# The start addresses of the SBUF tiles that TensorE reads, moved to multiples of 512 bytes

## The chip, the cores and the metric

One core of one Trainium2 chip runs the whole program. The metric is the device time of one execution in microseconds (us). Three runs of the kernel before took 2045.38, 2045.49 and 2047.89 us, with a median of 2045.49 us.

## The reference

A two-layer encoder trunk on 512 positions and 1024 channels, all in float32. One layer, cut to what matters here:

```python
hn = rmsnorm(x, norm_mix_g[l])
proj = hn @ w_in[l]                              # columns split among four mixers and four gates
ya, yb, yc, yd = mixer_a(...), mixer_b(...), mixer_c(...), mixer_d(...)
gates = sigmoid(gl.reshape(b, s, N_BRANCH, D_MODEL) + gate_bias[l])
merged = sum(gates[:, :, i] * (y_i @ w_proj_i[l]))
x = x + merged @ w_out[l]
hn = rmsnorm(x, norm_mlp_g[l])
x = x + square(relu(hn @ w_mlp1[l])) @ w_mlp2[l]  # 1024 -> 4096 -> 1024
```

Mixer A is dense attention, B a bidirectional linear recurrence, C windowed attention with a sink, D dilated windowed attention. A last RMSNorm ends the trunk.

## The kernel before

Activations lie in SBUF with channels on the 128 partitions and the 512 positions along the free dimension. A product of 1024 by 128 weights with the 512 positions is a chunk. Every weight matrix comes from HBM in chunks of 128 x 1024 numbers (`wload`, L102); ScalarE rounds a chunk to fp32r (`whi`, L118) and VectorE takes the remainder (`wlo`, L127). Activations are split the same way: `xh` and `xl` are the normalised input of the layer or of its MLP, `mh` and `ml` the merged mixers, the two `h` tiles of a quarter (`h0`, `h1`) the hidden MLP quarter, `y` with its two halves the output of a mixer. For each 128 contraction rows `mm3` then issues three matmuls, at full width of 512 columns:

```python
mm(ps, sh, mh, start=(k == 0), stop=False)    # L177  whi, high half of the activations
mm(ps, sh, ml, start=False, stop=False)       # L178  whi, low half
mm(ps, sl, mh, start=False, stop=(k == n - 1))  # L179  wlo, high half
```

The first operand after `ps` is the stationary one (128 columns of 4 bytes, 512 bytes of a partition, loaded by an LDWEIGHTS that the trace shows as PEld). The second is the moving one (512 columns, 2048 bytes of a partition). `several` (L193 to L195) issues the same three for two chunks in turns. An MLP chunk or an output chunk has 8 contraction steps, so 24 matmuls; a stage of 8 such chunks has 192.

The order of the work is fixed by the program. A layer has phase 1 (30 chunks with `xh` and `xl` moving, with rotary, convolution and recurrence beside them), the attention stages A, C and D, whose steps are merged with the gate chunks GL (`xh`, `xl` moving) and the branch projections PR (`y` moving) by `merge`, then the output stage OUT (`mh`, `ml` moving), then the MLP: the first half M1 (`xh`, `xl` moving) and the second half M2 (`h` moving) by quarters in the order M1(0) M1(1) M2(0) M1(2) M2(1) M1(3) M2(2) M2(3). In layer 1 the last two chunks of M2(3) run at half width (L1235 to L1237). Attention reads `Q`, `P`, `VV`, `VD`, `Qd` as stationary and `K`, `PT0`, `PT1`, `ptd`, `Kd` as moving tiles; its transposes (L835, L976) move the identity, a part of the constants `cs`, against a block of `P`.

Where a tile begins is set by the order and the sizes of the pools and tiles. The constants begin at byte 16512 of the partition. The tiles of pool `cp` before the weight pools are `cs`, `ve`, `ones`, `acc`, `rb`, `d_hb`, `d_lgb`, `d_sp`, `d_nsp` and `d_nsink`, the last one 64 bytes. They end at byte 27200, which is 53 x 512 + 64. Behind them lie the pools of `raw`, `whi` and `wlo`, `xh` and `xl`, the small tiles (`sm`), and the pools of the stages. Every chunk tile is a multiple of 512 bytes, so whatever offset the first has, the rest of that run of pools has too.

Of the kernel before, what the change touches and what calls it, by code (L numbers as in the profile page):

```python
# [11 lines left out]
F32 = mybir.dt.float32  # L12
F32R = mybir.dt.float32r
# [7 lines left out]
DM, S, DEPTH, HD = 1024, 512, 2, 64  # L21
EPS = 1e-6
NEG = -1e30
KD = DM // 128
# [51 lines left out]
class Body:  # L76
# [138 lines left out]
        return self.mm3(ps, self.wst(hl), self.xmv, KD, step)  # L215


    def smt(self, n, tag):
        return self.sm.tile([128, n], F32, tag=tag, name=tag)

    def rsqrt(self, v, n, tag):

# [54 lines left out]
    def setup(self):  # L277
        nc = self.nc
        cp = self.cp
        self.cs = cp.tile([128, NC_], F32, name="cs")  # L280
        self.ve = cp.tile([128, DEPTH * NV + 8], F32, name="ve")
        self.ones = cp.tile([128, 128], F32, name="ones")
        nc.sync.dma_start(out=self.ve, in_=self.vec)
        nc.vector.memset(self.ones, 1.0)
        nc.scalar.copy(self.ones[0:1, 0:1], self.ones[0:1, 0:1])
        self.ident = self.cs[:, C_ID:C_ID + 128]
        nl = DEPTH
        self.xh = self.xgp.tile([128, KD, S], F32R, name="xh")
        self.xl = self.xgp.tile([128, KD, S], F32R, name="xl")
        self.acc = cp.tile([128, S], F32, name="acc")  # L290
        self.rb = cp.tile([128, S], F32, name="rb")
        self.d_hb = cp.tile([128, nl, 32], F32, name="d_hb")
        self.d_lgb = cp.tile([128, nl, 16], F32, name="d_lgb")
        self.d_sp = cp.tile([128, nl, 8], F32, name="d_sp")
        self.d_nsp = cp.tile([128, nl, 8], F32, name="d_nsp")
        self.d_nsink = cp.tile([128, nl, 8], F32, name="d_nsink")

    def derive(self):
        nc = self.nc
        nv = nc.vector  # L300
        vv = self.ve[:, 0:DEPTH * NV].rearrange("p (l n) -> p l n", l=DEPTH)
        ts = nv.tensor_scalar
        ts(out=self.d_hb, in0=vv[:, :, V_GB:V_GB + 32], scalar1=0.5, scalar2=None, op0=ALU.mult)
        ts(out=self.d_lgb, in0=vv[:, :, V_LGB:V_LGB + 16], scalar1=0.5, scalar2=None, op0=ALU.mult)
        ts(out=self.d_nsink, in0=vv[:, :, V_SINK:V_SINK + 8], scalar1=-1.0, scalar2=None, op0=ALU.mult)

        n = DEPTH * 8
        sh = lambda t: t.rearrange("p (l n) -> p l n", l=DEPTH)
        lam = self.smt(n, "spl")
        ts(out=sh(lam), in0=vv[:, :, V_LAM:V_LAM + 8], scalar1=1.0, scalar2=None, op0=ALU.mult)  # L310
        mx, u, d, s, s2, p = (self.smt(n, "sp" + c) for c in "mudsqp")
        nv.scalar_tensor_tensor(out=mx, in0=lam, scalar=-1.0, in1=lam, op0=ALU.mult, op1=ALU.min)
        nc.scalar.activation(out=u, in_=mx, func=AF.Exp)
        ts(out=d, in0=u, scalar1=2.0, scalar2=None, op0=ALU.add)
        nv.reciprocal(out=d, in_=d)
        nv.tensor_tensor(out=s, in0=u, in1=d, op=ALU.mult)
        nv.tensor_tensor(out=s2, in0=s, in1=s, op=ALU.mult)
        ts(out=p, in0=s2, scalar1=1.0 / 17.0, scalar2=None, op0=ALU.mult)
        for k in (15, 13, 11, 9, 7, 5, 3):
            nv.scalar_tensor_tensor(out=p, in0=p, scalar=1.0 / k, in1=s2, op0=ALU.add, op1=ALU.mult)  # L320
        nv.scalar_tensor_tensor(out=p, in0=p, scalar=1.0, in1=s, op0=ALU.add, op1=ALU.mult)
        ts(out=mx, in0=lam, scalar1=-1.0, scalar2=0.0, op0=ALU.mult, op1=ALU.max)
        nv.scalar_tensor_tensor(out=p, in0=p, scalar=2.0, in1=mx, op0=ALU.mult, op1=ALU.add)
        ts(out=self.d_sp, in0=sh(p), scalar1=4.0, scalar2=None, op0=ALU.mult)
        ts(out=self.d_nsp, in0=sh(p), scalar1=-4.0, scalar2=None, op0=ALU.mult)

    def v(self, l, i):
        return self.ve[:, l * NV + i:l * NV + i + 1]
# [68 lines left out]
    def phase1(self, l):  # L397
        nc, p1 = self.nc, self.p1
# [3 lines left out]
        self.nrs8 = self.mixp.tile([128, 4], F32, tag="nrs8", name="nrs8")  # L402
        self.rs8p = self.mixp.tile([128, 4], F32, tag="rs8p", name="rs8p")
        self.rqs = self.mixp.tile([128, 4, 8], F32, tag="rqs", name="rqs")
        self.VV = self.mixp.tile([128, 4, 4, 128], F32R, tag="VV", name="VV")
        self.yB = self.y0p.tile([128, 2, 4, S], F32R, tag="y", name="yB")
        self.qsA = self.drp.tile([8, 128, S], F32, tag="qsA", name="qsA")
# [53 lines left out]
            self.derive()  # L461

        rd = self.drp.tile([S], F32, tag="rd", name="rd")
        self.roff = self.mixp.tile([128, 4], F32, tag="roff", name="roff")
        nc.sync.dma_start(out=rd.rearrange("(o n) -> o n", o=1), in_=row)
        nc.sync.dma_start(out=self.roff, in_=rd.rearrange("(p r) -> p r", r=4))
        self.conv_b(l, 0, X["bx", 0])
# [75 lines left out]
    def conv_b(self, l, f, ps):  # L543
        p1, nv, ns = self.p1, self.nc.vector, self.nc.scalar
        v = lambda i: self.v(l, i)
        bx = p1.tile([128, S + 4], F32, tag="bx", name="bx", bufs=4)
        nv.memset(bx[:, 0:2], 0.0)
        nv.memset(bx[:, S + 2:S + 4], 0.0)
        nv.tensor_tensor(out=bx[:, 2:S + 2], in0=ps, in1=self.rb, op=ALU.mult)
        xc = p1.tile([128, S], F32, tag="xc", name="xc", bufs=4)  # L550
        if f == 0:
            self.xcs, self.xch, self.bdone = {}, {}, set()
        self.xcs[f] = xc

        def tap(j):
            if j == 0:
                ns.activation(out=xc, in_=bx[:, 0:S], func=AF.Identity, scale=v(V_CW + f), bias=v(V_CB + f))
            else:
                nv.scalar_tensor_tensor(
                    out=xc, in0=bx[:, j:j + S], scalar=v(V_CW + 4 * j + f), in1=xc, op0=ALU.mult, op1=ALU.add  # L560
                )

        self.bq.append(lambda: tap(0))
        self.bq.append(lambda: (tap(1), tap(2)))
        self.bq.append(lambda: tap(3))
        if f < 2:
            self.bq.append(lambda: self.split_b(f))
# [321 lines left out]
    def attn_d(self, l, y):  # L889
        nc, ap = self.nc, self.ap  # L890
        nv, ns = nc.vector, nc.scalar
        QK, OG, PO = {}, {}, {}
        ML = [ap.tile([128, 4, 2, 4], F32, tag=f"ML{g}", name=f"ML{g}", bufs=1) for g in range(3)]
        mld = self.drp.tile([3, S, 8], F32, tag="mld", name="mld")
        wd = self.drp.tile([12, S], F32, tag="wd", name="wd")
        steps = []
# [11 lines left out]
        def step(g, h, u, first, last):  # L908
# [22 lines left out]
            def exps():  # L931
                ps = st["s"]
                P = st["P"] = ap.tile([128, S], F32, tag="P", name="P", bufs=4)
                if g == 0:
                    for w in range(2):
# [7 lines left out]
                        )  # L943
                        nm = ML[0][:, c, 0, h:h + 1]
                        nv.tensor_scalar(
# [3 lines left out]
                            out=Pw, in_=Pw, func=AF.Exp, scale=self.rs8[:, c:c + 1], bias=nm,  # L949
                            accum_out=ML[0][:, c, 1, h:h + 1],  # L950
                        )
                else:
# [5 lines left out]
                    nv.tensor_reduce(out=m, in_=P3, axis=AX.X, op=ALU.max, negate=True)  # L958
                    nv.tensor_tensor(out=ML[g][:, :, 0, h], in0=m, in1=self.rs8p, op=ALU.mult)
                    for r in range(4):  # L960
                        ns.activation(
                            out=P3[:, r], in_=P3[:, r], func=AF.Exp, scale=self.rs8p[:, r:r + 1],
                            bias=ML[g][:, r, 0, h:h + 1], accum_out=ML[g][:, r, 1, h:h + 1],
                        )
# [156 lines left out]
    def layer(self, l):  # L1121
# [27 lines left out]
            self.merge(self.attn_d(l, yD), self.fill(l, 2, yC), *MG[2])  # L1149
            self.merge(self.attn_d_end(yD), (next(fill) for _ in range(FN)), E1 + E2 + 1 + 2 * E3, FN)  # L1150
        mhp = pool(es_r, f"mh{l}", side="right")
        self.mh = mhp.tile([128, KD, S], F32R, name="mh")
        self.ml = mhp.tile([128, KD, S], F32R, name="ml")
        self.run(fill)
        es_mix.close()

# [21 lines left out]
        hp = pool(es_m, f"h{l}")  # L1178
        tp = pool(es_m, f"t{l}", 2)
        r2 = xp.tile([128, S], F32, name="r2")  # L1180
        H = {}

        def m1(q):
            H[q] = [hp.tile([128, KD, S], F32R, tag=f"h{z}", name=f"h{z}", bufs=2) for z in range(2)]
            early = self.several([("M1", 0, c) for c in range(2)], self.xmv, (6,)) if q == 0 else []
            for c in range(KD):
                if early:
                    ps = early.pop(0)
                else:
                    hl = self.take("M1", q, c)  # L1190
                    ps = self.wide()
                    self.run(self.proj8(hl, ps))
                if q == 0 and c == 3:
                    pv = self.misc()
                    nc.tensor.matmul(pv, self.ones, self.acc)
                    nv.tensor_scalar(out=r2, in0=pv, scalar1=1.0 / DM, scalar2=EPS, op0=ALU.mult, op1=ALU.add)
                    nv.reciprocal(out=r2, in_=r2)
                r = tp.tile([128, S], F32, tag="r", name="r")
                ns.activation(out=r, in_=ps, func=AF.Relu)
                nv.scalar_tensor_tensor(out=r, in0=ps, scalar=0.0, in1=r, op0=ALU.max, op1=ALU.mult)  # L1200
                self.split(r, H[q][0][:, c], H[q][1][:, c])
# [19 lines left out]
        def last(h):  # L1221
# [70 lines left out]
            store(1, 0, KD)  # L1292

        m1(0)
        m1(1)
        m2(0)
# [181 lines left out]
```

## Time and profile before

| | before |
|---|---|
| median of 3 runs | 2045.49 us |
| the profiled execution | 2045.1 us |
| its span, first to last instruction | 2043.3 us |
| mean granted clock of TensorE | 0.996 |
| TensorE matmul busy (PE) | 2023.1 us, 99% |
| weight loads busy (PEld) | 1664.0 us, 81% |
| VectorE (DVE), ScalarE (ACT) busy | 1270.7 us, 62%; 975.0 us, 48% |

The profiled execution's span leaves 1.8 us of its time outside. A matmul in these rows has a modelled end and overlaps the next one, so the duration of one is longer than the distance from its start to the next start. The rate of TensorE is read from the length of a stretch and the number of matmuls that begin in it.

### The profile page before, as it was taken

The page shows a single profiled execution, that of the slowest core. Times are in us where ns is not written, and L with a number is a line of the kernel's source. Part 1 is how long each engine was busy: PE and PEld are TensorE (multiplying, and loading weights), DVE is VectorE, ACT ScalarE, POOL GpSimd, SP SyncE. Part 2 cuts the span into 40 slices and gives each one's busy share as a digit, 9 for nine tenths or more (in the row PEclk, how much of TensorE's full clock was granted, in tenths as well). Part 3 has the DMA queues.
Part 4 walks back from the last instruction along what each step waited for, and adds up shares of the span by engine and source line. Part 5 has one row for each costly group of instructions (what it writes and reads, how often), then busy time and mean ns, then how long its engine had stood idle before and what let it go on. Part 6 is the DMA issues. An engine that isn't in the chain of part 4 may idle for free.

```text
span 2043.3 us, 25698 instructions
## 1 busy us (share of the span) xinstructions
PE 2023.1 (99%) x9752; PEld 1664.0 (81%) x9752; DVE 1270.7 (62%) x2274; ACT 975.0 (48%) x1701; POOL 0.2 (0%) x4
## 2 busy tenths in 40 slices
PE   9999999999999999999999999999999999999998
PEld 7888789887778888888878888898877888888886
DVE  6889775764466554444648897758544655444445
ACT  4357786854534332232323668768445344322322
POOL 0000000000000000000000000000000000000000
PEclk9999999999999999999999999999999999999999
DMA  5444325332233332323335552242322423333221
GB/s 189 148 151 144 119 68 154 105 125 82 54 119 130 96 101 93 101 91 98 121 106 165 155 165 93 69 154 95 128 73 58 161 93 100 96 93 103 93 94 62
DMA packets 87439, 227.03 MB, mean 111 GB/s; under 512 B 15098, under 2 KB 21370, under 8 KB 87316
## 3 DMA queue, kind: packets, MB, share of 16 engines
q1 hardware_dynamic: 84436, 221.20, 34.3%
q10 hardware_dynamic: 2880, 4.20, 0.6%
q8 instruction: 77, 1.26, 0.3%
q14 instruction: 46, 0.38, 0.1%
HBM read 201.08 MB, written 24.27 MB: 110 GB/s over the span
## 4 chain that ended last, share of the span: by engine, by line
PE 97%; DVE 1%; DMA 1%; ACT 1%; issue 0%; SPq 0%; DVEq 0%; ACTq 0%
PE ps_mm L177 14%; PE ps_mm L179 14%; PE ps_mm L178 14%; PE ps_t L177 7%; PE ps_t L179 7%; PE ps_t L178 7%; PE ps_s L177 6%; PE ps_s L179 6%; PE ps_s L178 6%; PE ps_o L856 2%; PE ps_t L835 2%; PE ps_s L796 1%; PE ps_s L797 1%; PE ps_o L1002 1%; PE ps_t L976 1%; PE ps_s L927 1%
## 5 line engine op out<-in xcount | busy, mean ns | idle before, releaser
L118 ACT CAST whi<-raw 128x1024 fp32r<-128x1024 f32 (+1 forms) x318 | 329.1, 1041 | 342.9 <-PE ps_mm L178 116.3
L127 DVE TENSOR_TENSOR wlo<-raw,whi 128x1024 fp32r<-128x1024 f32 (+1 forms) x318 | 384.8, 1214 | 98.2 <-ACT whi L118 95.5
L177 PE MATMUL ps_mm<-xh,whi 128*128 128x512 f32 x720 | 288.9, 401 | 0.0
L179 PE MATMUL ps_mm<-xh,wlo 128*128 128x512 f32 x720 | 282.4, 392 | 0.0
L178 PE MATMUL ps_mm<-xl,whi 128*128 128x512 f32 x720 | 282.1, 392 | 0.0
L177 PEld LDWEIGHTS ps_mm<-xh,whi 128*128 128x128 f32 x720 | 135.9, 189 | 32.5 <-issue 4.1
L179 PEld LDWEIGHTS ps_mm<-xh,wlo 128*128 128x128 f32 x720 | 135.9, 189 | 29.8
L178 PEld LDWEIGHTS ps_mm<-xl,whi 128*128 128x128 f32 x720 | 136.3, 189 | 26.9
L177 PE MATMUL ps_t<-xh,whi 128*128 128x512 f32 x368 | 143.6, 390 | 0.0
L178 PE MATMUL ps_t<-xl,whi 128*128 128x512 f32 x368 | 143.2, 389 | 0.0
L179 PE MATMUL ps_t<-xh,wlo 128*128 128x512 f32 x368 | 143.2, 389 | 0.0
L177 PE MATMUL ps_s<-xh,whi 128*128 128x512 f32 x352 | 138.5, 394 | 0.0
L179 PE MATMUL ps_s<-xh,wlo 128*128 128x512 f32 x352 | 137.0, 389 | 0.0
L178 PE MATMUL ps_s<-xl,whi 128*128 128x512 f32 x352 | 137.0, 389 | 0.0
L845 DVE TENSOR_TENSOR PT<-ps_t,PT 128x512 fp32r<-128x512 f32 (+2 forms) x128 | 75.1, 586 | 64.6 <-ACT PT L842 56.4
L829 ACT ACTIVATE P<-P,al 128x512 f32<-128x512 f32 (+2 forms) x128 | 82.7, 646 | 16.8 <-DVE al L828 15.6
L842 ACT CAST PT<-ps_t 128x512 fp32r<-128x512 f32 (+2 forms) x128 | 63.9, 501 | 47.6 <-PE ps_o L856 43.9
L719 DVE TENSOR_TENSOR gt<-ps_mm,rb 128x512 f32<-128x512 f32 x54 | 37.2, 688 | 78.3 <-PE ps_mm L179 77.9
L177 PEld LDWEIGHTS ps_t<-xh,whi 128*128 128x128 f32 x368 | 69.1, 188 | 17.3 <-issue 3.0
L179 PEld LDWEIGHTS ps_t<-xh,wlo 128*128 128x128 f32 x368 | 69.1, 188 | 14.3
L178 PEld LDWEIGHTS ps_t<-xl,whi 128*128 128x128 f32 x368 | 69.1, 188 | 14.2
L177 PEld LDWEIGHTS ps_s<-xh,whi 128*128 128x128 f32 x352 | 66.1, 188 | 14.9 <-issue 1.4
(423 smaller groups left out, 4228.7 us busy)
## 6 DMA issues: line engine op xcount, KB each, us to landing
raw<-in_w_dram SPq DMA_DIRECT2D x314, 512.0 KB, 3.5
qsA<-stk SPq DMA_DIRECT2D x32, 128.0 KB, 2.3
qsC<-stk SPq DMA_DIRECT2D x32, 128.0 KB, 2.3
K<-ks SPq DMA_DIRECT2D x16, 256.0 KB, 6.1
Q<-qsA SPq DMA_DIRECT2D x16, 256.0 KB, 3.7
Q<-qsC SPq DMA_DIRECT2D x16, 256.0 KB, 5.3
qD<-stkf SPq DMA_DIRECT2D x24, 128.0 KB, 2.2
kD<-stkf SPq DMA_DIRECT2D x24, 128.0 KB, 2.3
```

What stands on the lines that cost most here:

```text
L118: self.nc.scalar.copy(hi[:, s], self.raws[i][:, s])
L127: self.nc.vector.tensor_tensor(out=lo[:, s], in0=raw[:, s], in1=hi[:, s].bitcast(F32), op=ALU.subtract)
L177: mm(ps, sh, mh, start=(k == 0), stop=False)
L178: mm(ps, sh, ml, start=False, stop=False)
L179: mm(ps, sl, mh, start=False, stop=(k == n - 1))
L719: nv.tensor_tensor(out=g, in0=ps, in1=self.rb, op=ALU.mult)
L796: nc.tensor.matmul(ps[:, 0:n], qq, Kt[j][:, 0, b0 * 128:b1 * 128], start=True, stop=False)
L829: ns.activation(out=P[:, 0:n], in_=P[:, 0:n], func=AF.Copy, scale=ls)
L835: nc.tensor.transpose(pt[:, b * 128:(b + 1) * 128], P[:, b * 128:(b + 1) * 128], self.ident)
L842: ns.copy(st["dst"][0], st["src"])
L845: nv.tensor_tensor(out=st["dst"][1], in0=st["src"], in1=st["dst"][0].bitcast(F32), op=ALU.subtract)
L856: nc.tensor.matmul(o, a, b, start=(n_ == 0), stop=(n_ == len(mm) - 1))
```

## The change

No instruction is added, removed or moved, no operand changes its shape, and each instruction waits for the same semaphores with the same values as before. Only addresses change:

- `d_nsink` leaves pool `cp` for the pool `sm`, so that everything behind `cp` begins 64 bytes lower.
- The tiles of `derive` (the `sp` ones, used once) get one buffer instead of three; `roff` moves and is padded, `bx` and `ML2` are padded, so that the tiles behind them start at multiples of 512 bytes.
- `mh`, `ml` and the `h` tiles ask for an alignment of 512 bytes.

```diff
-    def smt(self, n, tag):
-        return self.sm.tile([128, n], F32, tag=tag, name=tag)
+    def smt(self, n, tag, bufs=3):
+        return self.sm.tile([128, n], F32, tag=tag, name=tag, bufs=bufs)
...
-        self.d_nsink = cp.tile([128, nl, 8], F32, name="d_nsink")
+        self.d_nsink = self.sm.tile([128, nl, 8], F32, name="d_nsink", bufs=1)
...
-        lam = self.smt(n, "spl")
+        lam = self.smt(n, "spl", 1)
...
+        self.roff = self.mixp.tile([128, 4], F32, tag="roff", name="roff", padded_shape=[128, 120])
...
-        bx = p1.tile([128, S + 4], F32, tag="bx", name="bx", bufs=4)
+        bx = p1.tile([128, S + 4], F32, tag="bx", name="bx", bufs=4, padded_shape=[128, S + 32])
...
-        ML = [ap.tile([128, 4, 2, 4], F32, tag=f"ML{g}", name=f"ML{g}", bufs=1) for g in range(3)]
+        pad = lambda g: [128, 8 if g == 2 else 4, 2, 4]
+        ML = [ap.tile([128, 4, 2, 4], F32, tag=f"ML{g}", name=f"ML{g}", bufs=1, padded_shape=pad(g)) for g in range(3)]
...
-        self.mh = mhp.tile([128, KD, S], F32R, name="mh")
-        self.ml = mhp.tile([128, KD, S], F32R, name="ml")
+        self.mh = mhp.tile([128, KD, S], F32R, name="mh", align_bytes=512)
+        self.ml = mhp.tile([128, KD, S], F32R, name="ml", align_bytes=512)
...
-            H[q] = [hp.tile([128, KD, S], F32R, tag=f"h{z}", name=f"h{z}", bufs=2) for z in range(2)]
+            H[q] = [hp.tile([128, KD, S], F32R, tag=f"h{z}", name=f"h{z}", bufs=2, align_bytes=512) for z in range(2)]
```

What this gives, as the start of the tile modulo 512 bytes, from the two programs' allocations:

| tile | read by TensorE as | before | after |
|---|---|---|---|
| `whi`, `wlo` | stationary (moving for the values, VAC and VD) | 64 | 0 |
| `xh`, `xl` | moving (stationary for VAC and VD) | 64 | 0 |
| `h0`, `h1` | moving, M2 | 192 in layer 0, 416 in layer 1 | 0 |
| `mh`, `ml` | moving, OUT | 480 | 0 |
| `y` of the four mixers | moving, PR | 448 | 0 |
| `Q`, `P` of A and C; `K`, `PT0`, `PT1` | stationary; moving | 448 | 0 |
| `VV` | stationary | 416 | 0 |
| `Qd`, `P` of D; `Kd`, `ptd` | stationary; moving | 320 | 0 |
| `VD` | stationary | 448 | 0 |
| `cs` (identity) | moving, transposes | 128 | 128 |
| `acc`, `ones` | both | 0 | 0 |

A slice of 128 columns of weights or of 512 positions is 512 or 2048 bytes long, so each slice has the offset of its tile. Three small stationary tiles (the norm columns `ny`, `kc` and `sq`) still begin elsewhere.

## Rows read from the trace of the kernel before

**Rows 1.** The page: span, busy time of each engine, granted clock by slice.

```profile
span 2043.3 us, 25698 instructions
...
PE 2023.1 (99%) x9752; PEld 1664.0 (81%) x9752; DVE 1270.7 (62%) x2274; ACT 975.0 (48%) x1701; POOL 0.2 (0%) x4
...
PEclk9999999999999999999999999999999999999999
```

**Rows 2.** The page: the chain that ended last, shares of the span by engine.

```profile
PE 97%; DVE 1%; DMA 1%; ACT 1%; issue 0%; SPq 0%; DVEq 0%; ACTq 0%
```

**Rows 3.** Busy time by stretch: start:end, length, busy (count) by engine, clock, DMA.

```profile
797.27:840.80 43.53, 43.53 (x193) 36.04 (x192) 20.79 (x24) 16.24 (x22) 0.00 (x0) 1.00 0.28 85
840.81:885.59 44.78, 44.78 (x193) 36.04 (x192) 20.25 (x24) 9.56 (x11) 0.00 (x0) 1.00 0.32 106
1762.50:1807.30 44.80, 44.80 (x193) 36.04 (x192) 20.25 (x24) 9.56 (x11) 0.00 (x0) 1.00 0.34 106
1807.31:1850.86 43.55, 43.55 (x193) 36.04 (x192) 20.79 (x24) 16.22 (x22) 0.00 (x0) 1.00 0.27 85
619.56:664.53 44.97, 44.97 (x193) 36.16 (x192) 29.21 (x38) 18.37 (x25) 0.00 (x0) 1.00 0.31 94
1629.58:1674.55 44.97, 44.97 (x193) 36.15 (x192) 29.20 (x38) 18.37 (x25) 0.00 (x0) 1.00 0.28 92
129.57:162.20 32.63, 32.63 (x145) 27.02 (x144) 29.39 (x40) 24.51 (x32) 0.00 (x0) 1.00 0.56 170
```

**Rows 4.** Timeline of TensorE where M1(2) begins and ends in layer 0.

```profile
797.04 0.39 PE L179 MATMUL ps_t<-h,wlo 128*128 128x512 f32 x1
797.27 0.39 PE L177 MATMUL ps_mm<-xh,whi 128*128 128x512 f32 x1
...
840.58 0.39 PE L179 MATMUL ps_s<-xh,wlo 128*128 128x512 f32 x1
840.80 0.40 PE L177 MATMUL ps_t<-h,whi 128*128 128x512 f32 x1
```

**Rows 5.** Timeline of TensorE in attention A of layer 0, one turn of the fill.

```profile
301.49 0.40 PE L177 MATMUL ps_mm<-xh,whi 128*128 128x512 f32 x1
301.73 0.40 PE L178 MATMUL ps_mm<-xl,whi 128*128 128x512 f32 x1
...
302.88 0.49 PE L835 MATMUL ps_t<-cs,P 128*128 128x128 f32 x3
```

**Rows 6.** The page: groups of matmuls of L177 to L179 on `xh`, `xl`, and transposes.

```profile
L177 PE MATMUL ps_mm<-xh,whi 128*128 128x512 f32 x720 | 288.9, 401 | 0.0
...
L177 PE MATMUL ps_t<-xh,whi 128*128 128x512 f32 x368 | 143.6, 390 | 0.0
...
L177 PE MATMUL ps_s<-xh,whi 128*128 128x512 f32 x352 | 138.5, 394 | 0.0
```

**Rows 7.** Groups of TensorE instructions: the transposes of attention A and C.

```profile
L835 PE MATMUL ps_t<-cs,P 128*128 128x128 f32 x416 | 66.3, 272 | 0.5 <-DVE PT L845 0.5
```

More of the change, by code (lines that the diff above doesn't have):

```diff
@@ L308, in derive @@
         sh = lambda t: t.rearrange("p (l n) -> p l n", l=DEPTH)
-        lam = self.smt(n, "spl")
+        lam = self.smt(n, "spl", 1)
         ts(out=sh(lam), in0=vv[:, :, V_LAM:V_LAM + 8], scalar1=1.0, scalar2=None, op0=ALU.mult)
-        mx, u, d, s, s2, p = (self.smt(n, "sp" + c) for c in "mudsqp")
+        mx, u, d, s, s2, p = (self.smt(n, "sp" + c, 1) for c in "mudsqp")
         nv.scalar_tensor_tensor(out=mx, in0=lam, scalar=-1.0, in1=lam, op0=ALU.mult, op1=ALU.min)
@@ L463, in phase1 @@
         rd = self.drp.tile([S], F32, tag="rd", name="rd")
-        self.roff = self.mixp.tile([128, 4], F32, tag="roff", name="roff")
         nc.sync.dma_start(out=rd.rearrange("(o n) -> o n", o=1), in_=row)
```

## The prediction

> **What bounds the kernel now.** I read the page first. TensorE is busy for 2023.1 of 2043.3 us, 99%, and every slice shows the full granted clock, which is the upper of its two levels, 2.4 GHz [rows 1]. The chain that ended last is TensorE for 97% of the span, with 1% each for VectorE, ScalarE and DMA [rows 2]. So only what changes the pace of TensorE's own instruction stream moves the time. VectorE and ScalarE, at 62% and 48%, can gain or lose a few per cent by their new addresses without a result, since TensorE covers them.
>
> The second view is the busy time by stretch [rows 3], which gives the pace. Each of the first six stretches holds exactly one stage of 192 full-width matmuls (its 192 weight loads count them; the matmul count has one more, which runs in from the stage before). The start and the end of the first stretch are seen in the timeline: it goes from the first matmul on `xh` to the first on `h` [rows 4]. Length divided by 192 is the distance from start to start:
>
> - M1(2) of layer 0 and M1(3) of layer 1, moving tiles `xh`, `xl`: 43.53 and 43.55 us, 226.7 and 226.8 ns.
> - M2(1) of layer 0 and M2(1) of layer 1, moving tiles `h`: 44.78 and 44.80 us, 233.2 and 233.3 ns.
> - OUT of both layers, moving tiles `mh`, `ml`: 44.97 us, 234.2 ns.
>
> One column per cycle would be 512 / 2.4 = 213.3 ns. All six stretches show the clock at 1.00, TensorE has no idle time in them, and the weight loads are busy for the same 36.04 to 36.16 us. The instructions have the same shape. The last row of the group is a piece of phase 1 with `xh`, `xl` moving: 32.63 us for 144 matmuls, 226.6 ns, although VectorE is busy for 29.39 of them and DMA for a share of 0.56. So load on the other engines and on DMA does not set the pace, and the tile that is read does.
>
> What distinguishes the tiles is their offset in a block of 512 bytes, as the table of the change has it. The weights begin at 64 everywhere. `xh`, `xl` also begin at 64, and this is the fast pair. `h` begins at 192 or 416, `mh` at 480, and these are slower by 6.5 and 7.5 ns. I conclude that the pair of addresses costs time: least where the moving tile and the next weights start at equal offsets, more where they differ.
>
> **The change part by part.** There is one effect to price, in four places. I take equal offsets as the thing that counts, so after the change M2, OUT and PR should go at the pace that M1 has now.
>
> *M2.* Seven full stages (four in layer 0, three in layer 1) and six of the eight chunks of the last one: 7.75 stages. Each loses 44.78 - 43.53 = 1.25 us [rows 3], 9.7 us in all. The half-width matmuls of the end I leave at nothing: 96 of them, at most 0.6 us at 6.5 ns each.
>
> *OUT.* Two stages, each 44.97 - 43.54 = 1.43 us: 2.9 us.
>
> *The projections of mixer D.* They run in long groups with no attention between them: 96 matmuls at 448 against 64. I price them as M2, 6.5 ns each: 0.6 us.
>
> *The attention stages.* Here GL and PR chunks come in turns of six matmuls between attention matmuls. One such turn of `xh` takes 302.88 - 301.49 = 1.39 us, 231.7 ns each [rows 5], 5.0 ns above M1 although its own offsets are equal. I read this as the pace having to settle again after attention's tiles at 448 and 416. It concerns 1152 GL matmuls (three branches, 8 chunks of 24, two layers), 576 of PR and 128 value matmuls at full width: 1856. All of it back would be 9.3 us, nothing back 0. Whether a turn still has to settle when every tile is aligned the trace cannot say, since no turn has all its neighbours equal. I take the middle, 4.6 us, and keep both ends.
>
> *At nothing:* phase 1 and M1 (their pair is equal before and after), the transposes and the other float32 matmuls. Three transposes take 0.49 us [rows 5] with a mean duration of 272 ns [rows 7], so they start (490 - 272) / 2 = 109 ns apart, and two cycles for each of the 128 columns would be 106.7. Their identity begins at 128 and `P` at 448, so at that slower stream unequal offsets cost at most 2.3 ns. That `cs`, `ny`, `kc` and `sq` stay off a block's start therefore costs nothing. The waits and the order are the same, and the smaller number of buffers in `derive` frees nothing that anyone waits for.
>
> The sum is 9.7 + 2.9 + 0.6 + 4.6 = 17.8 us. It is made against the profiled execution, 2045.1 us, of which 1.8 lie outside the span and stay. That gives 2027.3; I say **2027 us**. The median of the runs is 0.4 us above the profiled execution, which is less than the step. With the two ends of the attention term the forecast goes from 2022.6 to 2031.9.
>
> **The rivals.**
>
> *No change: addresses are not the cause.* M1 and M2 differ in more than addresses: who writes to SBUF beside them, and which PSUM drains follow. Layer 0 and layer 1 have `h` at 192 and at 416 and yet the same 44.78 and 44.80 us, which speaks for this rival: a shift by 224 bytes moved nothing. Against it stand OUT, which is slower still, and phase 1 under heavy traffic, which is as fast as M1 [rows 3]. The time would be 2045. The Trainium skill is on its side: "TensorE: Matmul & The Clock Gate", section "Step-by-step: what each phase is for", says that TensorE has two independent read ports, so that loading the next weights takes no bandwidth from the running matmul, and the section "Back-to-back issue gap" gives N / 2.4 + 2.5 ns, 215.8 for 512 columns, wherever the operands lie. By that rule the sum would be 0. The trace does not agree: 226.7, 233.2 and 234.2 ns for the same instruction.
>
> *Deeper: the start of the block itself counts, and 64 is not the best start.* Then M1 is not at its floor either. The distance from 213.3 ns is 13.4 ns in M1, and 2.3 ns in the transposes. If aligned tiles bring the full-rate matmuls down to that, 11.1 ns go from about 7,060 of them (4,320 of `xh`, `xl` in L177 to L179 [rows 6], 192 of them in `several`, 1,488 of M2, 384 of OUT, 672 of PR), 78 us beyond the forecast: 1949. Half of it would be 1988. For it: no full-rate matmul in the trace reads a tile that begins at 0, so nothing excludes it. Against it: 226.7 ns equals 544 cycles to the decimal, 32 over 512 in phase 1 and in both layers, which looks like a floor of the pair.
>
> *Slower: it was the start at 64 that was good, not the equality.* `xh`, `xl` and the weights are the only large tiles at 64, so equality and 64 cannot be told apart in the long stretches. If both streams beginning at 0 meet as badly as in M2, the clean `xh` matmuls, 4,512 less the 1,152 of the attention stages, lose 6.5 ns each, 21.8 us, and nothing is won elsewhere: 2067. It decides as soon as M1 goes above 226.7 ns by more than M2 and OUT win, 12.6 us over 3,360 matmuls or 3.8 ns.
>
> **How the numbers follow.** The forecast gets 0.60, the deeper gain 0.14, no change 0.12, slower 0.14. A measurement of this kernel can tell 0.2%, 4.1 us, from no change. Faster is the forecast and the deeper gain, 0.74; same 0.12; slower 0.14. The forecast's own range is 2022 to 2032. To hold 8 in 10 the range takes in no change (up to 2050) and the half of the deeper gain that is nearer, down to 1980: 0.60 + 0.12 + about 0.08.
>
> **What would show it.** Right: M2 and OUT stages of 43.5 us like M1, M1 unchanged at 43.5, the turn of the fill between 1.36 and 1.39 us, weight loads still 36.0 us for each stage, VectorE and ScalarE busy as before. The deeper rival shows in M1: anything under 43.3 us. The slower one shows there too: M1 at 44.8. No change shows as M2 at 44.8. I am wrong in the term of attention alone if M2 and OUT fall as said and the total is off by up to 5 us. I am wrong in the cause if M2 and OUT go one way and the fill the other.

## The result and the profile after

| | before | after |
|---|---|---|
| median of 4 runs each, us | 2045.43 (2045.16 to 2047.89) | 2030.39 (2027.48 to 2033.12) |
| ratio, 95% interval | | 0.9926 [0.9915, 0.9938] |
| profiled execution, us | 2045.1 | 2027.48 |

The change saves 15.0 us by the medians, 0.74%. The forecast was 2027, and the median lies inside its own range of 2022 to 2032.

The page of the kernel after, its span, engines, granted clock and the chain that ended last (as [rows 1, 2]):

```profile
span 2025.7 us, 25698 instructions
...
PE 2005.4 (99%) x9752; PEld 1661.6 (82%) x9752; DVE 1270.8 (63%) x2274; ACT 974.7 (48%) x1701; POOL 0.2 (0%) x4
...
PEclk9999999999999999999999999999999999999999
...
PE 89%; DVE 5%; ACT 2%; issue 1%; DMA 1%; SPq 0%; DVEq 0%; ACTq 0%
```

The instructions are the same in number, and TensorE is busy for 17.7 us less. VectorE and ScalarE are as busy as they were, and so, within 0.2%, are the weight loads. TensorE's share of the chain reads 89% where it was 97%; what lies behind that was not followed up, and TensorE is busy for 99% of the span in both.

Busy time by stretch of the kernel after, columns as in [rows 3]: OUT of layer 0, then M2(0), M1(2) and M2(1) of layer 0, then M2 in layer 1.

```profile
617.78:661.29 43.51, 43.51 (x193) 36.05 (x192) 29.28 (x38) 18.38 (x25) 0.00 (x0) 1.00 0.31 101
749.25:792.76 43.51, 43.51 (x193) 36.04 (x192) 20.25 (x24) 9.55 (x11) 0.00 (x0) 1.00 0.34 108
792.77:836.28 43.51, 43.51 (x193) 36.04 (x192) 20.80 (x24) 16.22 (x22) 0.00 (x0) 1.00 0.28 87
836.29:879.80 43.51, 43.51 (x193) 36.04 (x192) 20.24 (x24) 9.55 (x11) 0.00 (x0) 1.00 0.35 108
1749.83:1793.34 43.51, 43.51 (x193) 36.05 (x192) 20.25 (x24) 9.58 (x11) 0.00 (x0) 1.00 0.34 108
```

All five stages now have one length. The windows end 0.01 us ahead of the next start, so a stage is 43.52 us and the pace 226.7 ns, whichever tile moves. In [rows 3] M2 stood at 44.78 and 44.80 us, OUT at 44.97, M1 at 43.53. The load of VectorE, ScalarE and DMA beside each stage has not changed.

The attention stages are another matter. TensorE's busy time by stretch in the kernel before (busy, count, clock, DMA share, GB/s): 24 matmuls on `yD`, and a turn of six on `yB`.

```profile
613.96:619.55 5.59, 5.59 (x25) 1.00 1.03 370
...
254.17:255.56 1.39, 1.39 (x7) 1.00 0.00 0
```

The same two places in the kernel after, and ahead of them a turn of six on `xh`, the place of [rows 5]:

```profile
300.18:301.56 1.38, 1.38 (x7) 1.00 0.47 42
252.99:254.37 1.38, 1.38 (x8) 1.00 0.00 0
612.34:617.77 5.43, 5.43 (x25) 1.00 1.03 353
```

The group of mixer D goes from 5.59 / 24 = 232.9 ns to 5.44 / 24 = 226.7. The turn on `yB` wins 0.01 to 0.02 us. The turn on `xh` lasts from 300.18 to 301.57, 1.39 us as in [rows 5], and gets nothing back.

One part of the profiled difference does not come from addresses. Two stretches of the kernel before, by the same view; the fourth number is the granted clock:

```profile
209.00:212.40 3.40, 3.40 (x9) 0.50 1.07 252
1052.10:1055.50 3.40, 3.40 (x10) 0.50 0.02 5
```

The second place in the kernel after:

```profile
1043.50:1046.90 3.40, 3.40 (x16) 1.00 0.00 0
```

In the profiled execution of before TensorE ran at the lower level, 1.2 GHz, in these two places: after a wait of 2.2 us ahead of attention, and in phase 1 of layer 1, shortly after the small matmuls of L431 that sum the squares of the heads. In that of after it went through the same places at 2.4 GHz, although its wait ahead of attention was 2.4 us. Matched matmul by matmul (the time from each start to the next, in one trace less the same in the other) each of the two stretches cost about 1.6 us: a matmul took 427 ns in them, and 224 to 236 ns at the same place after. (Both executions also end at the lower level, but in the last 8 us TensorE is busy for only 1.2 in either.) The slices of the page are too coarse to show them [rows 1]; the mean clocks, 0.996 against 0.998, do.

### The profile page after: what moved, and what is told of

Same layout as the page of the kernel before. It is cut to its first block, busy times and chain, and to the rows that moved or that the text cites. A ratio compares the mean times of both kernels' runs of the same rounds, so it can differ in the third digit from the quotient of the medians.

```text
span 2025.7 us, 25698 instructions
## 1 busy us (share of the span) xinstructions
PE 2005.4 (99%) x9752; PEld 1661.6 (82%) x9752; DVE 1270.8 (63%) x2274; ACT 974.7 (48%) x1701; POOL 0.2 (0%) x4
## 4 chain that ended last, share of the span: by engine, by line
PE 89%; DVE 5%; ACT 2%; issue 1%; DMA 1%; SPq 0%; DVEq 0%; ACTq 0%
PE ps_mm L177 13%; PE ps_mm L178 13%; PE ps_mm L179 13%; PE ps_t L177 6%; PE ps_t L179 6%; PE ps_t L178 6%; PE ps_s L177 6%; PE ps_s L179 6%; PE ps_s L178 6%; PE ps_o L856 2%; PE ps_t L835 2%; PE ps_s L796 1%; PE ps_s L797 1%; DVE wlo L127 1%; PE ps_o L1003 1%
## 5 line engine op out<-in xcount | busy, mean ns | idle before, releaser
L177 PE MATMUL ps_mm<-xh,whi 128*128 128x512 f32 x720 | 287.8, 400 | 0.0
L179 PE MATMUL ps_mm<-xh,wlo 128*128 128x512 f32 x720 | 280.9, 390 | 0.0
L177 PEld LDWEIGHTS ps_mm<-xh,whi 128*128 128x128 f32 x720 | 135.2, 188 | 32.2 <-issue 4.1
L179 PEld LDWEIGHTS ps_mm<-xh,wlo 128*128 128x128 f32 x720 | 135.3, 188 | 29.6
L177 PE MATMUL ps_t<-xh,whi 128*128 128x512 f32 x368 | 143.7, 390 | 0.0
L179 PE MATMUL ps_t<-xh,wlo 128*128 128x512 f32 x368 | 143.2, 389 | 0.0
L177 PE MATMUL ps_s<-xh,whi 128*128 128x512 f32 x352 | 138.5, 394 | 0.0
L179 PE MATMUL ps_s<-xh,wlo 128*128 128x512 f32 x352 | 137.1, 389 | 0.0
L177 PEld LDWEIGHTS ps_t<-xh,whi 128*128 128x128 f32 x368 | 69.1, 188 | 17.2 <-issue 3.0
L179 PEld LDWEIGHTS ps_t<-xh,wlo 128*128 128x128 f32 x368 | 69.1, 188 | 14.4
L177 PEld LDWEIGHTS ps_s<-xh,whi 128*128 128x128 f32 x352 | 66.1, 188 | 14.9 <-issue 1.4
```

## The experiments

Two theories were open. **Equality**: the distance between the offsets of the moving and the stationary tile sets the pace. **Start**: each tile has good and bad starts of its own. A third question was why the attention stages gave back so little. Distance means here the moving tile's offset less that of the stationary one, and a pair such as 64/0 names the two offsets in this order. Times of this section stand against runs of the kernel before on the same chip: a median of 2047.08 us (7 runs) for the kernels 1 to 4, and 2046.51 us (12 runs) for 5 to 8. Differences of two or three us between such medians should not be read: experiment 2, whose stages have the lengths of the change, lies 18.2 us below its before, and the change 15.0 below its own.

**1. The pace by offset, measured by itself.** The kernel after with 37 blocks of 49 matmuls added between OUT and the MLP of layer 0. They move slices of `xh` against slices of `whi` from shifted addresses into a PSUM tile that nothing reads.

```diff
+        for mo, so, n, m in [(0, 0, 512, 128), (4, 0, 512, 128), (8, 0, 512, 128), (16, 0, 512, 128),
...
+            ps = self.misc()
+            for j in range(49):
+                k = j % 7
+                nc.tensor.matmul(
+                    ps[0:m, 0:n], hi[:, k * 128 + so // 4:k * 128 + so // 4 + m],
+                    xf[:, k * 512 + mo // 4:k * 512 + mo // 4 + n], start=(j == 0), stop=(j == 49 - 1),
+                )
```

> The changed kernel with 37 blocks of 49 matmuls added between OUT and M1(0) of layer 0, whose results nothing reads. A block moves 512 columns of xh from one byte offset against 128 columns of a weight tile from another byte offset. Theory 1 (equal offsets modulo 512 count): 226.7 ns from start to start where the two offsets are equal, whichever they are (0/0, 64/64, 128/128, 448/448), and about 233 ns for every unequal pair, whether the moving or the stationary tile is the one that is off. Theory 2 (the start of the block counts): 0/0 alone is fast, equal pairs at 64, 128 or 448 are as slow as unequal ones, and pairs with one operand at 0 lie between. Theory 3 (the distance counts by degrees or with a shorter period): the pace changes step by step with the distance, or 256 is as good as 0. The blocks of 64 and 32 stationary columns tell what the 13.4 ns over 213.3 are: about 6.7 and 3.3 ns if they are paid per column of weights, 13.4 again if they are not. The time as a whole is about 410 us longer and says nothing.

TensorE by stretch, each from the tenth matmul of a block to the forty-sixth, 36 starts. Offsets, moving and stationary: 0 and 0; 4 and 0; 32 and 0; 64 and 0; 128 and 0; 256 and 0; 4 and 4; 64 and 64; 0 and 64; 0 and 256.

```profile
664.64:672.80 8.16, 8.16 (x37) 1.00 0.22 66
676.15:684.62 8.47, 8.47 (x37) 1.00 0.00 0
711.43:719.83 8.40, 8.40 (x37) 1.00 0.00 0
734.76:743.00 8.24, 8.24 (x37) 1.00 0.00 0
758.10:766.50 8.40, 8.40 (x37) 1.00 0.01 2
793.41:801.58 8.17, 8.17 (x38) 1.00 0.00 0
875.24:883.84 8.60, 8.60 (x37) 1.00 0.00 0
898.85:907.01 8.16, 8.16 (x37) 1.00 0.00 0
968.00:976.40 8.40, 8.40 (x37) 1.00 0.00 0
991.47:999.63 8.16, 8.16 (x37) 1.00 0.00 0
```

Divided by 36: 226.7 ns at 0/0, 64/64, 256/0 and 0/256, and so it was at 128/128, 192/192, 256/256 and 448/448 (226.6 to 226.9). Between 228.9 and 236.7 ns lay every other distance: 228.9 at 64/0 and 320/0, 233.3 at 128/0, 234.3 at 160/0, 236.7 at 496/0. Equality is right, with three corrections. The distance counts modulo 256, not 512, as theory 3 had left room for. And equal offsets help only on some boundary, since 4/4 costs 239 ns, more than any distance between round offsets. The third is the width. With 256 moving columns the equal pair 0/0 is not the faster one; here it is, then 128/0:

```profile
1059.88:1064.20 4.32, 4.32 (x39) 1.00 0.01 4
1066.06:1070.33 4.27, 4.27 (x38) 1.00 0.00 0
```

That is 120.0 and 118.6 ns. With 64 stationary columns, too, 128/0 costs no more than 0/0 (229.5 against 230.0 ns). The price belongs to 512 moving columns against 128 stationary ones.

These numbers also give the price of each stage in [rows 3]: `h` of layer 0 is at distance 128 (233.2 there, 233.3 here), OUT at 416, which is 160 modulo 256 (234.2 there, 234.3 here), and `h` of layer 1 at 352, which is 96 (233.3 in both). The shift by 224 bytes that moved nothing between the layers led from one distance of this price to another.

The 13.3 ns that stay over 512 / 2.4 are not a price per column: with 256 columns the pace at 0/0 was 120.0 ns and with 384 173.3, 32 cycles over either. Nor are they one per weight column: with 64 stationary columns 230.0 ns, with 32 231.7.

**2. All tiles at 64.** The large tiles, `mh`, `ml` and `h` of the kernel after begin at byte 64 of a block: `gap` pushes the whole run of pools up, and `off(pool, o)`, a helper of these experiments, takes an aligned tile and leaves out its first `o` bytes. It tells equality from a gift of byte 0.

```diff
+        self.gap = cp.tile([128, 16], F32, name="gap")
...
+        self.mh = off(mhp, 64, name="mh")
+        self.ml = off(mhp, 64, name="ml")
...
+            H[q] = [off(hp, 64, tag=f"h{z}", name=f"h{z}", bufs=2) for z in range(2)]
```

> The changed kernel with every tile moved to byte 64 of a block, the moving and the stationary ones alike. Theory 1 (equality counts): as the changed kernel, 2027 to 2033 us, M1, M2 and OUT stages all 43.5 us. Theory 2 (the start at byte 0 counts): M1 stays at 43.5, M2 and OUT go back to 44.8 and 45.0, 2040 us or more.

2028.84 us (2028.03 to 2034.36), ratio 0.9923 [0.9902, 0.9944]. OUT and M2(1) of layer 0, by stretch:

```profile
617.47:660.98 43.51, 43.51 (x193) 36.04 (x192) 29.27 (x38) 18.37 (x25) 0.00 (x0) 1.00 0.29 97
835.97:879.48 43.51, 43.51 (x193) 36.04 (x192) 20.24 (x24) 9.56 (x11) 0.00 (x0) 1.00 0.34 108
```

Byte 0 has nothing of its own.

**3. Only `h`, `mh` and `ml`, at 64 in the kernel before.** This is M2 and OUT alone, the 12.6 us of the first two terms.

```diff
-        self.mh = mhp.tile([128, KD, S], F32R, name="mh")
...
+        self.mh = off(mhp, 64, name="mh")
+        self.ml = off(mhp, 64, name="ml")
...
+            H[q] = [off(hp, 64, tag=f"h{z}", name=f"h{z}", bufs=2) for z in range(2)]
```

> The kernel before with only h0, h1, mh and ml moved, to byte 64, where its weights begin; attention tiles stay at 448, 416 and 320. Theory 1: M2 and OUT stages at 43.5 us, so 9.7 + 2.9 = 12.6 us less than before, 2033 us; what is left to the changed kernel is the attention part alone. Theory 2: no change, 2045 us.

2032.8 us (2030.55 to 2035.93), ratio 0.9936 [0.9920, 0.9952]; OUT of layer 0, M2 of layer 0 and of layer 1:

```profile
618.04:661.56 43.52, 43.52 (x193) 36.03 (x192) 29.12 (x38) 18.38 (x25) 0.00 (x0) 1.00 0.30 98
749.51:793.02 43.51, 43.51 (x193) 36.04 (x192) 20.24 (x24) 9.57 (x11) 0.00 (x0) 1.00 0.33 107
1752.88:1796.39 43.51, 43.51 (x193) 36.04 (x192) 20.24 (x24) 9.58 (x11) 0.00 (x0) 1.00 0.32 108
```

So these tiles carry most of it: 14.3 us by the medians, against 18.2 for experiment 2 in the same group of runs. Matched matmul by matmul in the traces, M2 and OUT win 12.8 us here, as they do in the change (9.9 and 2.9).

**4. The rest alone.** The kernel after without the alignment of `h`, `mh` and `ml`. They fall to 320 in layer 0 and 32 in layer 1, and to 480.

```diff
-        self.mh = mhp.tile([128, KD, S], F32R, name="mh", align_bytes=512)
-        self.ml = mhp.tile([128, KD, S], F32R, name="ml", align_bytes=512)
+        self.mh = mhp.tile([128, KD, S], F32R, name="mh")
+        self.ml = mhp.tile([128, KD, S], F32R, name="ml")
...
-            H[q] = [hp.tile([128, KD, S], F32R, tag=f"h{z}", name=f"h{z}", bufs=2, align_bytes=512) for z in range(2)]
+            H[q] = [hp.tile([128, KD, S], F32R, tag=f"h{z}", name=f"h{z}", bufs=2) for z in range(2)]
```

> The changed kernel without the alignment of h0, h1, mh and ml, which fall to 320 (layer 0), 32 (layer 1) and 480; everything else begins at byte 0. Theory 1: M2 and OUT stay at 44.8 and 45.0 us (M2 at 32 may differ, since a distance of 32 was not in the trace of before); the time is that of before less the attention part: 0.6 us for mixer D's projections and between 0 and 4.6 for the rest, 2040 to 2045 us. Theory 2 (byte 0 counts by itself for weights or xh): clearly below 2040, with M1 under 43.5 us.

2037.84 us (2036.93 to 2040.27), ratio 0.9961 [0.9947, 0.9976], faster than expected. OUT, M2(0) and M1(2) of layer 0, then M2 in layer 1:

```profile
618.31:663.11 44.80, 44.80 (x193) 36.07 (x192) 29.37 (x38) 18.38 (x25) 0.00 (x0) 1.00 0.29 96
751.09:795.04 43.95, 43.95 (x193) 36.06 (x192) 20.25 (x24) 9.58 (x11) 0.00 (x0) 1.00 0.33 107
795.05:838.61 43.56, 43.56 (x193) 36.05 (x192) 20.79 (x24) 16.20 (x22) 0.00 (x0) 1.00 0.26 86
1756.08:1800.88 44.80, 44.80 (x193) 35.99 (x192) 20.25 (x24) 9.56 (x11) 0.00 (x0) 1.00 0.33 106
```

The stage that came out otherwise is M2 of layer 0: 43.96 / 192 = 229.0 ns, the pace of experiment 1 at 64/0 and 320/0, since its new distance happens to be 320. Priced by distance the run comes out: M2 of layer 0 loses 4 x 0.44, that of layer 1 3.75 x 1.29, OUT 2 x 1.29, 9.2 us in all, over the 2028.84 of experiment 2 in the same runs 2038.0. I had not reckoned with a distance that costs a third. Against before, 9.2 us are won by the medians, and 6.7 by the two profiled executions, each with two stretches at the lower clock: the expected 2040 to 2045 was missed in part by M2 of layer 0 (3.3 us won) and in part by the scatter of the medians.

**5. The fast pair made unequal.** `xh` and `xl` of the kernel after 128 bytes up, all else in place. If addresses set the pace, M1 must now become the slow stage.

```diff
+        self.gap = self.xgp.tile([128, 32], F32, name="gap")
...
-        self.roff = self.mixp.tile([128, 4], F32, tag="roff", name="roff", padded_shape=[128, 120])
+        self.roff = self.mixp.tile([128, 4], F32, tag="roff", name="roff", padded_shape=[128, 88])
```

> The changed kernel with xh and xl moved by 128 bytes against everything else. If the distance of the moving tile to the next weights sets the pace (233.4 ns at 128 in the probe, 226.7 at 0), every long stretch on xh, xl slows to 233.3 ns: M1 stages from 43.5 to 44.8 us, M2 and OUT stay at 43.5. 3360 clean matmuls by 6.7 ns are 22 us, all 4512 are 30 us: 2050 to 2062 us. If the turns of six in the attention stages are set by something else than addresses, they stay at 231 ns and the lower end holds.

2051.6 us (2050.38 to 2053.34), ratio 1.0027 [1.0016, 1.0038], slower than before. M2(0), M1(2), M2(1) of layer 0:

```profile
759.31:802.84 43.53, 43.53 (x193) 36.04 (x192) 20.25 (x24) 9.58 (x11) 0.00 (x0) 1.00 0.32 108
802.85:847.63 44.78, 44.78 (x193) 36.04 (x192) 20.79 (x24) 16.21 (x22) 0.00 (x0) 1.00 0.26 85
847.64:891.16 43.52, 43.52 (x193) 36.04 (x192) 20.25 (x24) 9.57 (x11) 0.00 (x0) 1.00 0.34 107
```

The picture of [rows 3] turned round: M1 now has the 44.78 us that M2 had, and M2 the 43.53 of M1. The medians of the two kernels, from different groups of runs, lie 21.2 us apart. Matched matmul by matmul, the long groups on `xh` and `xl` lose 20.2 us over the kernel after (3,228 matmuls, 6.2 ns each), and the turns of up to 24 matmuls 3.3 us (1,284 matmuls, 2.5 ns each; 2.0 us of it in the attention stages). So the distance costs a short turn as well, but less than half of what it costs a long group.

**6. The identity aligned as well.** In the kernel after `cs` begins so that the identity is at 256. Does the turn on `xh` fail to settle because the transposes ahead of it read a shifted tile, or because it was interrupted at all?

```diff
+        self.d_lgb = cp.tile([128, DEPTH, 16], F32, name="d_lgb")
...
-        self.d_lgb = cp.tile([128, nl, 16], F32, name="d_lgb")
```

> The changed kernel with the constants tile moved from byte 128 to byte 256 of a block, so that the identity of the transposes too has a distance of 0 (modulo 256) to what is loaded beside it. Theory a (the transposes' unequal pair throws the following turn out of step): the turns of six on xh go from 230.8 towards 227 ns, up to 4 us less than the changed kernel. Theory b (any interruption throws the pair out of step, whatever its addresses): turns stay at 230.8 ns and the time is that of the changed kernel within 1 us.

2029.3 us (2028.59 to 2032.36), ratio 0.9920 [0.9908, 0.9933], no gain over the change. The 44 turns of six on `xh` take 231.5 ns a matmul at the median, against 231.6 after and 231.7 before. Experiment 1 shows the same without attention. Its block at 64/64 begins after a pause: 0.33 us pass from its first start to its second. Here are the six starts from the second on:

```profile
897.01:898.40 1.39, 1.39 (x7) 1.00 0.00 0
```

Six take 1.39 us, 231.7 ns each, the number of [rows 5]; from the tenth on it is 226.7. The other blocks at equal offsets and 512 by 128 columns, multiples of 32, needed five to eleven matmuls to settle, the one that alternates 0 and 256 in experiment 7 two. The block at 0/0 was the first of all and followed OUT without a pause, and it stood at 226.7 ns from its first start. A turn of six is over before most pairs have settled. What in the interruption throws the two streams out of step was not tried.

**7. What the distance acts on.** 23 more blocks as in experiment 1, with 48 matmuls: other distances, offsets that alternate from matmul to matmul, and float32 operands, which the trace shows as two passes.

```diff
+                m, s = mo[j % len(mo)] // 4, so[j % len(so)] // 4
+                a, b = hi[:, k * 128 + s:k * 128 + s + 128], xf[:, k * 512 + m:k * 512 + m + n]
+                if kind == "f":
+                    a, b = a.bitcast(F32), b.bitcast(F32)
```

> A second probe: 23 blocks of 48 matmuls whose results nothing reads, at the place of the first. (1) Period: distances 224, 288, 352 and 416 at the pace of -32, 32, 96 and 160 if the period is 256 bytes. (2) Only the distance counts: 64/128, 128/64, 192/64, 320/192, 448/64 and 64/448 at the pace of -64, 64, 128, 128, 128 and 128. (3) Whose weights: blocks whose moving offset alternates 0, 128 while the weights alternate 128, 0 have each matmul unequal to its own weights and equal to the next ones; 226.7 ns if the next weights count, 233 if its own do; the block that alternates alike gives the opposite. Alternating 0 and 256 gives 226.7 either way. (4) float32 blocks of 256 columns, two passes of half the column rate: 216 ns a pass at every distance, if the price falls due only where the moving tile streams at full rate. (5) 24/0, 32/32, 96/96 and 8/8 tell how fine an equal start must be: the first probe had 231 ns for 16/16 and 227 for 64/64.

36 starts each, as in experiment 1. Moving and stationary 128 and 64; moving 0, 128 with weights 128, 0 by turns; 0, 128 with 0, 128 by turns; float32 passes of 256 columns at 0/0 and at distance 64; 32 and 32; 8 and 8.

```profile
721.10:729.34 8.24, 8.24 (x37) 1.00 0.00 0
778.53:786.82 8.29, 8.29 (x38) 1.00 0.00 0
789.90:798.12 8.22, 8.22 (x38) 1.00 0.01 2
835.18:842.95 7.77, 7.77 (x38) 1.00 0.00 0
856.22:863.99 7.77, 7.77 (x37) 1.00 0.00 0
931.01:939.17 8.16, 8.16 (x37) 1.00 0.01 2
953.52:961.91 8.39, 8.39 (x37) 1.00 0.00 0
```

- Float32 passes take 215.8 ns at distances 0, 64, 128 and 192 alike. At half the stream rate the addresses have no price, as the prediction took it for the transposes.
- 32/32 and 96/96 are at the floor of 226.7 ns, 8/8 is at 233.1, 16/16 in experiment 1 at 231.1: of the equal starts tried, only those on a multiple of 32 are at the floor.
- 224, 288, 352 and 416 against 0 cost 233.3 to 234.2 ns, as 32, 96 and 160 do: the period is 256. The sign counts, too: 128/64 takes 228.9 ns, 64/128 233.3.
- By turns, 230 and 228 ns. If only the matmul's own weights counted, the second would be at 226.7; if only the next ones did, the first would. Neither is, so which load the moving stream meets stays open.

**8. `h`, `mh` and `ml` at 256, the rest at 0.**

```diff
+        self.mh = off(mhp, 256, name="mh")
+        self.ml = off(mhp, 256, name="ml")
...
+            H[q] = [off(hp, 256, tag=f"h{z}", name=f"h{z}", bufs=2) for z in range(2)]
```

> The changed kernel with h0, h1, mh and ml at byte 256 of a block, everything else at 0. If equality modulo 256 is enough: the changed kernel's time, 2027 to 2033 us, M2 and OUT stages at 43.5 us. If 512 is needed in a kernel's own sequence: M2 and OUT at 44.8 us and above, 2040 us or more.

2028.35 us (2027.18 to 2031.94), ratio 0.9916 [0.9902, 0.9929]; OUT and M2(1) of layer 0:

```profile
617.88:661.39 43.51, 43.51 (x193) 36.04 (x192) 29.27 (x38) 18.38 (x25) 0.00 (x0) 1.00 0.30 98
836.39:879.90 43.51, 43.51 (x193) 36.04 (x192) 20.25 (x24) 9.57 (x11) 0.00 (x0) 1.00 0.33 108
```

As good as the change in whole stages too: blocks of 512 are more than is needed. No version here beats the change by more than the runs scatter.

## Why the prediction was right, point by point

| term | forecast, us | measured, us |
|---|---|---|
| M2 | 9.7 | 9.9 |
| OUT | 2.9 | 2.9 |
| mixer D's PR and the attention stages | 0.6 + 4.6 | about 2.7 |
| sum | 17.8 | 15.5 |
| two stretches at 1.2 GHz, in the profiled execution of before alone | not priced | 3.1 |

*The bound and the cause* were read rightly. Weight loads, VectorE, ScalarE and DMA did not change, and TensorE's pace did. ("Every slice shows the full granted clock" read more into [rows 1] than a digit 9, for 90% or more, can tell: slices with a stretch at 1.2 GHz show it too.) The step from two kinds of stages to "equal offsets" was an inference from one fast pair. Experiments 2 and 5 are what shows it: equality at another byte gives the whole gain, and inequality makes the fast stage slow.

*M2 and OUT* came out as priced, since the trace of before held the pace that they would go to. The half-width matmuls, left at nothing, gave nothing, as the blocks of 256 columns have it. That the pairs priced there all lay at dear distances (96, 128 and 160 modulo 256) is luck: at 320 the same M2 stage loses 0.44 us and not 1.25 (experiment 4).

*The attention term* is the one that was mis-sized. "I take the middle, 4.6 us" was a choice between two bounds with no row that favoured it, and what came back is near the lower one. Over all turns of L177 to L179 in the attention stages and in mixer D I added up the time above 226.7 ns for each matmul. On `y` it fell from 3.7 to 1.6 us (0.6 of that is mixer D, as priced). The value matmuls fell from 0.8 to 0.2. On `xh` and `xl` it stayed as it was, to 0.2 us. These turns had equal offsets already; they pay for settling, and that was not bought off by aligning their neighbours. The nearest row was [rows 5] itself: a pair at equal offsets that is slow cannot be slow because of its own offsets, which spoke for the bound of nothing for its 1,152 matmuls.

*The agreement of the profiled executions* is partly luck. They differ by 17.6 us, almost the forecast 17.8, but 3.1 of it is the clock, and about 1.0 goes the other way in waits, half of it because attention starts later (the first `K`, `Q` matmul at 209.17 us instead of 208.70). The medians, 15.0 us apart, are the better measure of the addresses, and agree with the 15.5 of the terms.

*The rivals.* No change fell with M2 at 43.5 us. The rule that the prediction set beside it, of two independent read ports and N / 2.4 + 2.5 ns (the Trainium skill, "TensorE: Matmul & The Clock Gate", "Step-by-step: what each phase is for" and "Back-to-back issue gap"), has no term for addresses. It does not agree with full-rate streams of 512 columns here, 226.7 to 239.0 ns. It does agree with the float32 passes, 215.8 ns at every distance (experiment 7), if N is read as 512 cycles for 256 columns at half the rate. The deeper gain fell with M1 at 43.51 us: byte 0 is no better than 64. The slower rival fell with the same row, and experiment 2 shows why: neither 64 nor 0 is good by itself.

## What to carry to other kernels

Where TensorE is the bound and streams fp32r operands at full rate, 512 columns against 128, give the moving and the stationary tile the same start modulo 256 bytes, on a multiple of 32; here that was worth 2.8 to 3.2% of each long stage it touched. At 256 and 384 columns it is worth nothing: the value matmuls of these widths went from 117.0 to 118.6 and from 173.8 to 175.1 ns when their tiles, 32 bytes apart before, were aligned. Read the pace as stage length over matmul count and compare stages of the same shape: the longer one has a cause that busy shares don't show, because TensorE is at 99% in both. Short turns between other work pay for settling whatever the addresses are, and an unequal pair cost them 2 to 3 ns a matmul in place of 6.6, so price them at less than half of the long groups.

## What the runs showed of the hardware that was not expected

- With 512 columns and starts on multiples of 32, the distance modulo 256 sets the pace to about 1 ns, and it is not a matter of more or less: 64 costs 2.2 ns a matmul, 128 costs 5.6 to 6.6, 160 costs 7.6. Other starts do not keep to it: 496/0 and 0/16 have the same distance and take 236.7 and 233.3 ns, and the equal pair 4/4 takes 239.0.
- The floor of an aligned fp32r pair is N / 2.4 + 13.3 ns with 256, 384 and 512 columns alike. What these 32 cycles are stays open. At 256 columns the pair at distance 128 is below it, 118.6 against 120.0 ns.
- After a pause an equal pair needs five to eleven matmuls before it is at its floor (231.7 ns over the first six at 64/64).
- In single executions TensorE ran at 1.2 GHz after a pause or after small matmuls, at about 1.6 us a time, and in others not, at the same place of the same instruction stream. The four runs of the kernel after order by it: 2027.48, 2029.34, 2031.44 and 2033.12 us at a mean granted clock of 0.998, 0.997, 0.996 and 0.995. So it makes up much of the scatter of the runs.
